# A convolution whose last two channel blocks change PSUM pools, with a statistics step moved between their taps and weight splits held further back

## The chip, the cores and the metric

One core of a Trainium2 chip runs the whole program in one launch. The metric is device time in microseconds (us), the median of several runs. Stretches of the trace are given in us from the start of the profiled span.

## What is computed

Four layers, one after the other, on 256 tokens of width 1024, each followed by a gated feed-forward layer. Everything is float32 in and out; matrix products are done at near-float32 accuracy by splitting each operand into a high and a low part. The change lies in the last mixer, the "conformer" convolution:

```
def conformer_conv(h, w_pw1, b_pw1, w_dw, b_dw, ln_g, ln_b, w_pw2, b_pw2):
    a, gate = jnp.split(h @ w_pw1 + b_pw1, 2, axis=-1)
    u = a * jax.nn.sigmoid(gate)
    dw = lax.conv_general_dilated(u, w_dw[:, None, :], window_strides=(1,),
        padding=((CONV_WIDTH_2 - 1, 0),), ..., feature_group_count=D_MODEL) + b_dw
    mu, var = mean and variance of dw over the channels
    z = jax.nn.silu((dw - mu) * lax.rsqrt(var + EPS) * ln_g + ln_b)
    return z @ w_pw2 + b_pw2
```

The convolution has 31 taps for each of 1024 channels, which lie as 8 blocks (k = 0 to 7) of 128 channels on the partitions and 256 tokens along the free axis.

## The kernel before, in words

The stage (`conformer`) works through a list of steps, `ORDER`: `p` steps project two channel blocks into banks of the pool `acc` (four banks), gate them on ACT (L1193) and DVE (L1195) into a tile `u` and split `u` into `uh` and `ul` (L170 on ACT, L171 on DVE). `c` steps convolve two blocks. Of the 31 taps of a block some (`PE_TAPS`) are done on PE: for each tap a diagonal matrix with the tap's weight, in high and low parts, is the stationary operand, and three matmuls of 128x256 (L335 to L337, high x high, high x low, low x high) sum into one bank of the pool `pw`, two banks. The diagonals are made by ACT (L1140, one 128x128 activation for each half) for blocks 0 to 6, and for block 7 by GpSimd (L1135, one `affine_select` for up to eight taps). They stand in a rotating pool of four tiles. Taps beyond the sixteenth use odd offsets and copies of `uh`, `ul` moved by one (L1222, L1223). The other taps run on DVE, one instruction a tap (L1243 for the first, L1245 for the rest), into `d`; at the end the PE bank is added to `d` (L1248), which sets the bank free.

`s` steps (`stat`) transpose two finished blocks of `d` on PE (L1254) into a bank of the pool `ptr` and take `bn_stats` on DVE (L1257). When all four are done, DVE aggregates (L1276) and adds EPS (`eps`, L1277), GpSimd takes the power -0.5 (L1278), DVE forms the negative mean (`mean`, L1279), and PE spreads both over the partitions into a bank `br` (L1282). Then, for pieces of one, one, two, two and two blocks, DVE multiplies and adds (L1290, L1291; the adds are `adds[0]` to `adds[4]`), ACT applies Silu (L1293) and casts the high part `zTh` (L170), and DVE forms the low part `zTl` (L171). Matmuls of 10 and 7 that compute nothing (L218) run on PE while it waits here.

The output projection (`outproj`) multiplies by `conv_w_pw2` in four chunks of two channel blocks; each chunk is one 1 MB transfer into `raw` (L144, queued on SP, three buffers), and is split in four pieces of 128x512 into `hi` (L164, ACT) and `lo` (L166, DVE), three buffers each. Chunks 0 and 1 go through all banks first; chunks 2 and 3 are the tail, bank by bank, and each finished bank is added to `x` (L411). `self.hold` says behind which DVE instruction the low part of each piece may be issued, for chunks 0, 1 and 2.

Each engine's queue runs in order; the order is fixed when the program is built, from the order of the code, the dependencies, and a lead (`high_priority(offset=...)`): the normalization steps have a lead of 800 (`FIRST`), the splits of chunk 0 of 120, of the other chunks of 1.

Of the kernel before, what the change touches and what calls it, by code (L numbers as in the profile page):

```python
# [17 lines left out]
P = 128  # L18
D = 1024
S = 256  # L20
# [11 lines left out]
TUNE = [(150, 4), (1, 4), (400, 4), (1, 4), (1, 4), (1, 4), (400, 4), (1, 4)]  # L32
XBC = (4, 5, 0, 1, 2, 3)
FIRST = 800
ORDER = "p0 c01 p1 c23 s0 p2 c45 s1 p3 c67 s2 s3"
MORDER = "s0 p0 s1 v0 p1 n1 v1 s2 s3 v2 v3"
PE_TAPS = [13] * 6 + [16, 20]


def f32(ap):  # L40
    return ap.bitcast(F32)


def T(t):
    return slice(t * P, (t + 1) * P)
# [12 lines left out]
class Net:  # L58
# [1084 lines left out]
    def conformer(self, after):  # L1143
# [3 lines left out]
        with self.stage("conf") as sp, self.stage("confp") as pp:  # L1147
            s1 = lambda shape, name, dt=F32, **kw: sp.tile(list(shape), dt, name=name, **kw)
# [55 lines left out]
            def conv(ks):  # L1204

                bs, rest = {}, {}
                if ks[0] == 0:
                    with self.tc.issue_after(self.joint[0]), self.tc.issue_after(self.joint[1]):
                        for i in range(2):
                            n = 16 - i  # L1210
                            self.split(self.whl_dw[:, i, :n, 0], self.whl_dw[:, i, :n, 1], self.wdw[:, i::2])
                for k in ks:
                    u, uh, ul = us[k]
                    n_odd = max(0, PE_TAPS[k] - 16)
                    taps = [list(range(0, 2 * min(PE_TAPS[k], 16), 2)), list(range(1, 2 * n_odd, 2))]
                    rest[k] = [n for n in range(TAPS) if n not in taps[0] + taps[1]]
                    moved = [(uh, ul)]
                    if n_odd:

                        uh1 = sp.tile([P, H + S], F32R, tag="uh1", name="uh1", bufs=1)  # L1220
                        ul1 = sp.tile([P, H + S], F32R, tag="ul1", name="ul1", bufs=1)
                        nc.scalar.copy(uh1[:, :H + S - 1], f32(uh[:, 1:]))  # L1222
                        nc.scalar.copy(ul1[:, :H + S - 1], f32(ul[:, 1:]))  # L1223
                        moved.append((uh1, ul1))
                    b = bs[k] = self.bank("pw", (P, S))
                    left = PE_TAPS[k]
                    for odd in range(2):
                        for t0 in range(0, len(taps[odd]), 8):
                            ts = taps[odd][t0:t0 + 8]
                            with self.tc.issue_after(self.joint[0]):  # L1230
                                dg = self.diags(pp, ts, k)
                            for n, tap in enumerate(ts):
                                c = slice(tap - odd, tap - odd + S)
                                self.mm3W(b, dg[:, 2 * n], dg[:, 2 * n + 1], moved[odd][0][:, c], moved[odd][1][:, c], left == PE_TAPS[k], left == 1)
                                left -= 1
                for n in range(TAPS):
                    for k in ks:
                        if n >= len(rest[k]):
                            continue
                        u, tap, dk = us[k][0], rest[k][n], d[:, k, :]  # L1240
                        w = self.wdw[:, tap, k:k + 1]
                        if n == 0:
                            nc.vector.tensor_scalar(dk, u[:, tap:tap + S], w, self.bdw[:, k:k + 1], op0=ALU.mult, op1=ALU.add)  # L1243
                        else:
                            nc.vector.scalar_tensor_tensor(dk, u[:, tap:tap + S], w, dk, op0=ALU.mult, op1=ALU.add)  # L1245
                with self.tc.high_priority(offset=FIRST if 7 in ks else 0):
                    for k in ks:
                        nc.vector.tensor_add(d[:, k, :], d[:, k, :], bs[k])  # L1248

            def stat(i):  # L1250
                bt = self.bank("ptr", (P, 2, 2, P))
                for j in range(2):
                    for t in range(2):
                        ins = nc.tensor.transpose(bt[:, t, j, :], d[:, 2 * i + j, T(t)], self.ident).ins  # L1254
                with self.tc.high_priority(offset=FIRST if i == 3 else 0):
                  for t in range(2):
                    nc.vector.bn_stats(stats[:, t, i, :], bt[:, t].rearrange("p j l -> p (j l)"))  # L1257
                return ins

            for step in ORDER.split():  # L1260
                if step[0] == "p":
                    proj(int(step[1]))
                elif step[0] == "c":
                    conv([int(x) for x in step[1:]])
                else:
                    turned = stat(int(step[1]))
# [3 lines left out]
            with self.tc.high_priority(offset=FIRST):  # L1270
                with self.tc.issue_after(turned):
                    self.warm(10, "ptr")
                s2 = lambda name, n=1: sp.tile([P, 2, n], F32, tag=name, name=name, bufs=1)
# [3 lines left out]
                eps = nc.vector.tensor_scalar(rm, mv[:, :, 1:2], EPS, None, op0=ALU.add).ins  # L1277
                nc.gpsimd.tensor_tensor(r, rm, self.nhalf[:, :2].rearrange("p (t o) -> p t o", o=1), op=ALU.pow)  # L1278
                mean = nc.vector.scalar_tensor_tensor(rm, mv[:, :, 0:1], -1.0, r, op0=ALU.mult, op1=ALU.mult).ins  # L1279
# [5 lines left out]
            k, adds = 0, []  # L1285
# [11 lines left out]
            for t in range(2):  # L1297
                nc.vector.tensor_add(self.x[t], self.x[t], bp)

            self.hold = [((), (eps, eps, mean, mean)), ((), (adds[1], adds[2], adds[3], adds[3])), ((), (adds[4],) * 4)]  # L1300
            self.outproj(a["conv_w_pw2_2"][0], lambda k, t: (zTh[:, k, T(t)], zTl[:, k, T(t)]), list(range(8)), after, ahead=1, ahead0=120)

    def late_params(self):
# [111 lines left out]
```

## Time and profile before

| | us |
|---|---|
| median of three runs | 1290.64 |
| the three runs | 1293.62, 1290.4, 1290.64 |
| the profiled execution, its own time | 1293.15 |
| its span in the profile | 1291.4 |
| PE busy in the span | 1271.0 |
| DVE busy | 916.0 |
| ACT busy | 768.5 |

The median is what a version is judged by; the profiled execution is one more run, in which 1.75 us lie outside the span. The shares by engine are over all four layers; the conformer takes the stretch from about 978 to 1098 us of the span.

### The profile page before, as it was taken

How to read it: one execution, taken by the hardware profiler on the slowest of the kernel's cores; microseconds unless marked ns; L12 is line 12 of the kernel's file. 1: busy time of each engine (PE TensorE's matmuls, PEld its weight loads, DVE VectorE, ACT ScalarE, POOL GpSimd, SP SyncE). 2: the span in 40 equal slices, each digit the busy share in tenths (PEclk: the TensorE clock that was granted, in tenths of full speed). 3: DMA queues.
4: the chain of work that ended last, by engine and by line, in shares of the span. 5: the costliest groups of instructions: out<-in, count | busy, mean ns of one | idle time of the engine just before them, and what ended most of it. 6: DMA issues, size and time to landing. Idle time of an engine off the chain costs nothing.

```text
span 1291.4 us, 19316 instructions
## 1 busy us (share of the span) xinstructions
PE 1271.0 (98%) x7188; PEld 1094.1 (85%) x7188; DVE 916.0 (71%) x1882; ACT 768.5 (60%) x1758; POOL 55.0 (4%) x106
## 2 busy tenths in 40 slices
PE   9999999999999999999999999999999999999997
PEld 8888878888888867888888888888889998888886
DVE  6966665767764987866746787777557998777643
ACT  6773554666653876666634445666447995666642
POOL 3000000400000000000000000000000010000000
PEclk9999999999999999999999999999999999999999
DMA  8436344766563433766554545656673304655560
GB/s 256 152 113 209 130 173 153 230 196 196 194 235 101 168 98 100 228 196 192 182 202 158 199 145 190 186 184 191 217 238 118 112 2 147 208 183 182 181 222 35
DMA packets 150543, 219.62 MB, mean 170 GB/s; under 512 B 6634, under 2 KB 119426, under 8 KB 150450
## 3 DMA queue, kind: packets, MB, share of 16 engines
q1 hardware_dynamic: 148528, 213.43, 50.9%
q0 software_dynamic: 1920, 4.96, 1.4%
q8 instruction: 56, 0.92, 0.3%
q14 instruction: 37, 0.30, 0.1%
q10 hardware_dynamic: 2, 0.00, 0.0%
HBM read 217.33 MB, written 1.05 MB: 169 GB/s over the span
## 4 chain that ended last, share of the span: by engine, by line
PE 90%; DVE 6%; ACT 3%; issue 1%; POOL 0%; POOLq 0%; DVEq 0%; ACTq 0%
PE acc L342 18%; PE acc L343 9%; PE acc L330 9%; PE acc L385 9%; PE acc L389 9%; PE acc L386 9%; PE pw L342 5%; PE acc L331 5%; PE pw L343 2%; PE acc L337 2%; PE acc L336 2%; PE acc L335 2%; PE ptr L258 2%; DVE lo L166 1%; PE pw L337 1%; PE pw L335 1%
## 5 line engine op out<-in xcount | busy, mean ns | idle before, releaser
L166 DVE TENSOR_TENSOR lo<-raw,hi 128x512 fp32r<-128x512 f32 (+2 forms) x800 | 514.2, 683 | 168.1 <-ACT hi L164 166.7
L164 ACT CAST hi<-raw 128x512 fp32r<-128x512 f32 (+2 forms) x800 | 448.6, 617 | 228.4 <-PE acc L389 84.9
L342 PE MATMUL acc<-xT,hi 128*128 128x512 f32 x1024 | 359.6, 396 | 0.0
L343 PE MATMUL acc<-xT,lo 128*128 128x256 f32 x1024 | 287.7, 281 | 0.0
L342 PEld LDWEIGHTS acc<-xT,hi 128*128 128x128 f32 x1024 | 192.1, 188 | 45.3
L343 PEld LDWEIGHTS acc<-xT,lo 128*128 128x128 f32 x1024 | 193.5, 189 | 0.2
L386 PE MATMUL acc<-lo,hTh 128*128 128x512 f32 x352 | 137.2, 390 | 0.0
L385 PE MATMUL acc<-hi,hTh 128*128 128x512 f32 x352 | 137.0, 389 | 0.0
L389 PE MATMUL acc<-hi,hTl 128*128 128x512 f32 x352 | 113.5, 389 | 0.0
L331 PE MATMUL acc<-hi,xT 128*128 128x512 f32 (+2 forms) x288 | 108.8, 378 | 0.2 <-DVE xT L171 0.2
L330 PE MATMUL acc<-hi,xT 128*128 128x512 f32 (+2 forms) x288 | 108.2, 376 | 0.0
L330 PE MATMUL acc<-lo,xT 128*128 128x512 f32 (+2 forms) x288 | 108.1, 375 | 0.0
L342 PE MATMUL pw<-xT,hi 128*128 128x512 f32 x256 | 89.8, 395 | 0.0
L459 DVE TENSOR_TENSOR s<-s,acc 128x256 f32<-128x256 f32 x128 | 53.3, 417 | 50.9 <-ACT s L458 50.8
L335 PE MATMUL acc<-xT,hi 128*128 128x256 f32 x288 | 81.8, 284 | 0.0
L337 PE MATMUL acc<-xT,lo 128*128 128x256 f32 x288 | 81.7, 284 | 0.1
L336 PE MATMUL acc<-xT,hi 128*128 128x256 f32 x288 | 81.7, 284 | 0.0
L385 PEld LDWEIGHTS acc<-hi,hTh 128*128 128x128 f32 x352 | 66.1, 188 | 13.9
L389 PEld LDWEIGHTS acc<-hi,hTl 128*128 128x128 f32 x352 | 66.1, 188 | 13.6
L386 PEld LDWEIGHTS acc<-lo,hTh 128*128 128x128 f32 x352 | 66.1, 188 | 13.5
L458 ACT COPY s<-acc 128x256 f32<-128x256 f32 x128 | 47.3, 369 | 45.1 <-PE acc L343 45.1
L343 PE MATMUL pw<-xT,lo 128*128 128x256 f32 x256 | 71.8, 280 | 0.0
(432 smaller groups left out, 2004.3 us busy)
## 6 DMA issues: line engine op xcount, KB each, us to landing
raw<-w_in_even SPq DMA_DIRECT2D x22, 1024.0 KB, 5.2
raw<-w_down SPq DMA_DIRECT2D x22, 1024.0 KB, 5.0
raw<-ffn_w_down SPq DMA_DIRECT2D x22, 1024.0 KB, 5.1
raw<-w_gate SPq DMA_DIRECT2D x20, 1024.0 KB, 5.4
raw<-w_up SPq DMA_DIRECT2D x20, 1024.0 KB, 5.6
raw<-ffn_w_gate SPq DMA_DIRECT2D x20, 1024.0 KB, 5.4
raw<-ffn_w_up SPq DMA_DIRECT2D x20, 1024.0 KB, 5.4
raw<-conv_w_pw SPq DMA_DIRECT2D x12, 1024.0 KB, 5.4
```

The costliest lines, as they stand in the source:

```text
L164: nc.scalar.copy(fl(hi)[:, c], fl(raw)[:, c])
L166: nc.vector.tensor_sub(fl(lo)[:, c], fl(raw)[:, c], f32(fl(hi)[:, c]))
L330: return [mm(out, lh, wh, start=first, stop=False).ins, mm(out, lh, wl, start=False, stop=False).ins, mm(out, ll, wh, start=False, stop=la ...
L331: mm(out, ll, wh, start=False, stop=last).ins]
L335: mm(out, wh, xh, start=first, stop=False)
L336: mm(out, wh, xl, start=False, stop=False)
L337: return mm(out, wl, xh, start=False, stop=last).ins
L342: mm(out.rearrange("p a s -> p (a s)"), wh, self.xx[:, k].rearrange("p a s -> p (a s)"), start=first, stop=False)
L343: mm(out[:, 0, :], wl, self.xx[:, k, 0, :], start=False, stop=last)
L385: done.append(nc.tensor.matmul(b, lh, hi[:, j, cs], start=st, stop=False).ins)
L386: done.append(nc.tensor.matmul(b, lh, lo[:, j, cs], start=False, stop=False).ins)
L389: done.append(nc.tensor.matmul(banks[t][h], ll, hi[:, j, cs], start=False, stop=sp).ins)
```

## The change

Four edits. The PE sums of blocks 6 and 7 go to the pool `acc` instead of `pw`. The statistics of blocks 4 and 5 (`s2`) are no longer a step after `c67`; they are traced between the PE taps of block 6 and those of block 7, and their `bn_stats` get the lead of 800 too. Block 7 has 21 PE taps instead of 20, so one tap fewer on DVE. The low parts of chunk 0 of the next weights are held behind `eps`, `mean`, `adds[1]`, `adds[1]` instead of `eps`, `eps`, `mean`, `mean`, and the first of chunk 1 behind `adds[2]` instead of `adds[1]`.

```
-ORDER = "p0 c01 p1 c23 s0 p2 c45 s1 p3 c67 s2 s3"
+ORDER = "p0 c01 p1 c23 s0 p2 c45 s1 p3 c67 s3"
-PE_TAPS = [13] * 6 + [16, 20]
+PE_TAPS = [13] * 6 + [16, 21]
...
-                    b = bs[k] = self.bank("pw", (P, S))
+                    b = bs[k] = self.bank("pw" if k < 6 else "acc", (P, S))
...
+                    if k == 6:
+                        stat(2)
...
-                with self.tc.high_priority(offset=FIRST if i == 3 else 0):
+                with self.tc.high_priority(offset=FIRST if i >= 2 else 0):
...
-            self.hold = [((), (eps, eps, mean, mean)), ((), (adds[1], adds[2], adds[3], adds[3])), ((), (adds[4],) * 4)]
+            self.hold = [((), (eps, mean, adds[1], adds[1])), ((), (adds[2], adds[2], adds[3], adds[3])), ((), (adds[4],) * 4)]
```

## Rows read from the trace of the kernel before

**Rows 1.** The page: busy time by engine, then the chain's shares by engine.
```profile
PE 1271.0 (98%) x7188; PEld 1094.1 (85%) x7188; DVE 916.0 (71%) x1882; ACT 768.5 (60%) x1758; POOL 55.0 (4%) x106
...
PE 90%; DVE 6%; ACT 3%; issue 1%; POOL 0%; POOLq 0%; DVEq 0%; ACTq 0%
```
**Rows 2.** Waits, 1052 to 1099: who waited for whom; us in total, times, longest.
```profile
ACT uh L170 <- DVE u L1195: 2.5, 1, 2.5
...
PE pw L335 <- DVE d L1248: 1.6, 1, 1.6
```
**Rows 3.** PE's timeline, 1053 to 1089: start, length, engine, line, operation, [idle before].
```profile
1053.63 0.36 PE L335 MATMUL pw<-uh,diag 128*128 128x256 f32 x1 [1.57 <-DVE d L1248]
...
1058.56 0.51 PE L337 MATMUL pw<-uh,diag 128*128 128x256 f32 x2 [0.44 <-ACT diag L1140]
...
1067.18 0.28 PE L335 MATMUL pw<-uh,diag 128*128 128x256 f32 x1
...
1067.54 1.11 PE L1254 MATMUL ptr<-ident,d 128*128 128x128 f32 x8
...
1071.90 0.61 PE L1282 MATMUL pw<-ident,rm 128*128 128x128 f32 x4
...
1075.21 0.51 PE L385 MATMUL acc<-hi,zTh 128*128 128x512 f32 x1 [1.14 <-ACT zTh L170]
...
1088.62 0.39 PE L386 MATMUL acc<-lo,zTh 128*128 128x512 f32 x1
```
**Rows 4.** The chain that ended last, 1050 to 1060: start, length, what.
```profile
1053.41 0.41 DVE d L1248
...
1055.36 0.48 DVE d L1245
1055.84 0.41 DVE u L1195
...
1056.27 0.43 ACT uh L170
...
1056.72 1.28 ACT L1201
...
1058.22 0.30 ACT diag L1140
```
**Rows 5.** ACT's timeline, 1052 to 1069: diagonals of block 6, casts of weights.
```profile
1052.47 1.26 ACT L1140 ACTIVATE diag<-ident,whl_dw 128x128 fp32r<-128x128 f32 x4
...
1058.13 3.90 ACT L1140 ACTIVATE diag<-ident,whl_dw 128x128 fp32r<-128x128 f32 x13
...
1064.67 4.26 ACT L164 CAST hi<-raw 128x512 fp32r<-128x512 f32 x8
```
**Rows 6.** DVE's timeline, 1035 to 1081.
```profile
1035.39 8.79 DVE L1245 SCALAR_TENSOR_TENSOR d<-u,wdw,d 128x256 f32<-128x256 f32 x22
...
1056.87 0.45 DVE L171 TENSOR_TENSOR ul<-u,uh 128x286 fp32r<-128x286 f32 x1
1057.24 9.37 DVE L1245 SCALAR_TENSOR_TENSOR d<-u,wdw,d 128x256 f32<-128x256 f32 x21
1066.71 0.42 DVE L1248 TENSOR_TENSOR d<-d,pw 128x256 f32<-128x256 f32 x1
1067.74 0.42 DVE L1248 TENSOR_TENSOR d<-d,pw 128x256 f32<-128x256 f32 x1 [0.61 <-PE pw L337]
1068.18 1.43 DVE L1257 BATCH_NORM_STATS2 stats<-ptr 128x6 f32<-128x256 f32 x4
...
1071.41 1.89 DVE L166 TENSOR_TENSOR lo<-raw,hi 128x512 fp32r<-128x512 f32 x3
1073.22 0.42 DVE L1290 TENSOR_TENSOR d<-d,pw 128x256 f32<-128x256 f32 x1
...
1080.48 1.89 DVE L166 TENSOR_TENSOR lo<-raw,hi 128x512 fp32r<-128x512 f32 x3
```
**Rows 7.** GpSimd's timeline: the first and the third of three selects.
```profile
1044.39 2.01 POOL L1135 TENSOR_SCALAR_AFFINE_SELECT diag<-whl_dw 128x2048 fp32r<-128x2048 f32 x1 [65.37 <-PE pw L337]
...
1056.82 1.45 POOL L1135 TENSOR_SCALAR_AFFINE_SELECT diag<-whl_dw 128x1024 fp32r<-128x1024 f32 x1 [6.32 <-PE pw L337]
```
**Rows 8.** DVE's groups from 1044.3 to 1046.6: busy us, mean ns.
```profile
L1245 DVE SCALAR_TENSOR_TENSOR d<-u,wdw,d 128x256 f32<-128x256 f32 x1 | 1.8, 1781 | 0.0
```
**Rows 9.** SP's queue: the last transfer of these weights; transfers by kind, us to landing.
```profile
1073.33 0.37 SPq L144 DMA_DIRECT2D raw<-conv_w_pw  x1
...
raw<-conv_w_pw SPq DMA_DIRECT2D x1, 1024.0 KB, 5.0
```

## The prediction

> **What bounds the kernel.** I read the page first: PE is busy 98% of the span and holds 90% of the chain that ended last; DVE holds 6% of it and ACT 3% [rows 1]. So a gain can only come where PE stands still, and only as far as PE gets back to work earlier. All that the change touches lies between 1044 and 1099 us, and there I read the waits [rows 2], PE's and DVE's timelines [rows 3, 6] and the chain itself [rows 4]. The reader is to see two places. At 1052 to 1053.63 PE stands for 1.57 us until DVE has added a finished sum out of a `pw` bank [rows 2, 3]. And from 1068.65, where the last transposes end, to 1075.21 PE has only the transposes' successors: statistics, the spread of mean and deviation, matmuls that compute nothing, and the wait for the first `zTh` [rows 3]. That is 6.6 us in which DVE, GpSimd and ACT set the pace. From 1075.21 on PE is full.
>
> **The bank of blocks 6 and 7.** With `acc` PE need not wait for the adds; the four `acc` banks are free by then, since the projection's sums leave them through L1193 and L1195. PE could start block 6 at 1052.0, 1.6 us earlier. Yet the chain does not run through that wait. It runs through DVE's add at 1053.41, on to `u` of block 7 at 1055.84, ACT's `uh` at 1056.27, a table load of 1.28 us and the diagonal at 1058.22 that PE waits for at 1058.56 [rows 3, 4]; DVE is the late one, and ACT stood 2.5 us for `u` [rows 2]. What is late next, once the bank is free: block 6 has 32 diagonals, 13 of them made after 1058.13, so 19 by 1053.73 [rows 5], that is 9.5 taps. A tap is three matmuls, 0.36 us (1067.18 to 1067.54 in [rows 3]). PE would have used them by 1052.0 + 9.5 x 0.36 = 1055.4 and then stand until block 7's `ul` at 1057.3 [rows 6] or the next diagonal. I take 0 for the bank. The other end: DVE must still finish. Its add of block 6 ends at 1066.71 + 0.42 = 1067.13 [rows 6]; it gets two `bn_stats` more before that (half of 1.43, +0.72), loses a tap (8.79 / 22 = 0.40, [rows 6]) and is held by a wider select (below, +0.14), which makes 1067.59. The last add began at 1067.74, after 0.61 us of idle time. So even a PE that is never late brings that add forward by no more than 0.15 us. The bank's value lies between 0 and 0.15 us.
>
> **The 21st tap.** PE gets 0.36 us more, on the chain, since DVE waits for PE at 1067.74; DVE's 0.40 us less is worth nothing there, as it was idle 0.61. GpSimd's third select grows from 1024 to 1280 columns. The 2048-column one took 2.01 us and this one 1.45 [rows 7], so 0.56 x 256 / 1024 = +0.14 us.
>
> **The select moves.** It waits for a diagonal tile that block 6's first eight taps set free. Those would end at 1052.0 + 24 x 0.12 + 0.3 = 1055.2 instead of 1056.8, so it runs from 1055.2 to 1056.8 with 1.45 + 0.14 us, ahead of `u` and `ul` of block 7 and no longer behind them. The first select ran from 1044.39 to 1046.40, and the DVE tap beside it took 1.78 us [rows 7, 8] where the normal pitch is 0.40. The tap in front of `u` (at 1055.36, [rows 4]) would then end at 1056.8 and `u` with it at 1057.2 instead of 1056.25: 0.95 us, or nothing, if the tap starts just ahead of the select; then the tap and the first-tap instruction between `u` and `ul` are held instead. With `ul` behind them the bounds are 0 and 1.4 us. I take 0.6, in between, because start times here agree to within 0.2 us and either order is open. DVE's own end does not move, for it loses this time to a select in both versions. The Trainium skill ("SBUF — State Buffer", Who interferes with whom) has a rule that speaks against this change: a DVE instruction with two SBUF inputs and a GpSimd instruction that reads SBUF exclude each other for the whole instruction, one with a single SBUF input is not held. By that rule the tap is held to the end and `u`, which reads PSUM and one SBUF operand, only by queueing behind it; the row of 1.78 us agrees. By it alone the term would be 0.95 to 1.4, which is the second rival.
>
> **The statistics step.** Four transposes (half of 1.11 us in [rows 3], 0.5) move from the end to PE's idle time after 1055.4, hidden by the wait for block 7's `ul`; if PE gets to them only later they cost up to 0.5 on the chain. `d` of blocks 4 and 5 is ready by 1053.82 [rows 4]. At the end two `bn_stats` remain. Today four run back to back from 1068.18 to 1069.61, the first two over the last two transposes, which end at 1068.65 [rows 3, 6]. Then they would run from 1068.70 to 1069.42: 0.2 us gained.
>
> **End of the convolution, summed:** last add +0.36 (tap) + 0.6 (select) + 0 (bank, transposes) - 0.35 (of the stalls of PE up to 1058.56: 108 matmuls at 0.12 make 12.9 us, and it took 13.9; a third of that 1.0 may close) = +0.6 us, between -0.15 and 0.36 + 1.4 + 0.5 = +2.3. Statistics -0.2.
>
> **The low parts held back.** Between `mean` and the first multiply three low parts run, to 1073.3; the multiply starts at 1073.22, though the spread it needs ended at 1071.90 + 0.61 = 1072.51 [rows 3, 6]. With one low part there the multiply can start at 1072.55: 0.67 us gained, bounds 0.6 and 0.7. The two others and the third of chunk 1 have smaller leads than the multiplies, adds and `zTl`, so they go where chunk 1's went, to 1080.48 [rows 6]: two low parts there end 1.2 us later, at 1081.7, less a shift of 0.27 = 1081.4. Chunk 0's `raw` buffer is free only then, and the transfer of chunk 3 waits for it: it was issued at 1073.33, when the last low part of chunk 0 had ended [rows 6, 9]. SP's queue behind it holds the next layer's weights. Issued at 1081.5 it lands 5.0 us later [rows 9], 1086.5; four casts of 0.53 [rows 5] and low parts of 0.63 [rows 6] behind them give chunk 3's third low part at about 1088.8. PE takes it in the first bank of the tail at 1088.62 [rows 3], or 1088.35 after the shift. So PE stands some 0.5 us. It is 0 if the two low parts find an earlier gap on DVE, and much more if they come later (third rival). I take 0.5.
>
> **Sum and forecast.** +0.6 - 0.2 - 0.67 + 0.5 = +0.2 us: on the profiled execution's own 1293.15 (span 1291.4 and 1.75 around it) 1293.4. That run lies 2.5 us above the median, beside one of the three; two lie at 1290.4 and 1290.6. Carried to the median: 1290.9 us. The forecast's own range is -1.0 (-0.15 - 0.2 - 0.67) to +1.9 (2.3 - 0.2 - 0.67 + 0.5): 1289.6 to 1292.5. A measurement of this kernel can tell about 0.3%, 3.9 us, from no change; all of this is less.
>
> **Rivals.** First, the bank wait counts: PE uses the time, the order on PE fits, chunk 3 is in time. For it speaks that 1.57 us is PE's longest wait here [rows 2]; against it the chain and DVE's end at 1067.59. It gives -1.0 us, 1289.6. Second, the select holds DVE for all of its length in front of `u`, and the transposes fall on the chain: +1.9 us, 1292.5; for it the 1.78 us row. Third, on the other side, late weights: should the two low parts of chunk 0 be put behind those of chunks 1 and 2 too, eight of 0.61 us = 4.9 us later, chunk 3 lands at 1091.4 and PE stands 0.5 + 4.9 = 5.4 us in the tail: 1290.64 - 0.3 + 5.4 = 1295.7. It decides from a release of chunk 0's `raw` at about 1085 on. Against it speaks their lead, 120 against 1. Fourth, the new order of instructions reaches further than these edits, into the next layer, and shortens PE's 6.6 us at 1068 to 1075 by more than half: -4 us, 1286.6; nothing in the rows shows how, since DVE, GpSimd and ACT do the same steps one after the other.
>
> **Chances.** Forecast 0.60, first rival 0.20, second 0.10, third 0.06, fourth 0.04. The first three lie within 0.3%: same 0.90, slower 0.06, faster 0.04. The range leaves out the last two and takes in the run at 1293.6 that the unchanged kernel shows: 1289.0 to 1293.6.
>
> **What would show it.** In the changed trace: no wait of PE for L1248 at 1052, but a new one between 1055 and 1058.5, for `uh`, `ul` or a diagonal; the third select near 1055, beside a DVE tap of over 1 us; the last L1248 0 to 2 us later than 1067.74; one low part between `mean` and the first L1290; the transfer of chunk 3 near 1081 instead of 1073, and a short wait of PE for `lo` or `hi` near 1088. The prediction is wrong if the last L1248 comes well before 1067.6, if chunk 3 is issued before 1076, or if the time leaves 1287 to 1294.5 us.

## The result

The changed kernel took 1301.5 us (median of 1301.92, 1301.5 and 1300.64) against 1290.64. The quotient of these medians is 1.0084; the ratio on record, which goes with the 95% interval of 1.0037 to 1.009 and is used from here on, is 1.0064. Run again later beside 22 runs of the kernel before, it gave 1.0058 [1.0041 to 1.0076]. The forecast of 1290.9 us and the range of 1289.0 to 1293.6 were wrong; the sign was that of the third rival, at another place.

In the profile PE holds 89% of the chain instead of 90% [rows 1]. Lines behind the new step stand two further on: L1248 of before is L1250, L1245 is L1247, L1257 is L1259. The waits of the changed kernel, 1052 to 1099 us (who waited for whom, total, times, longest), against [rows 2]:

```profile
DVE d L1250 <- PE acc L337: 4.3, 1, 4.3
ACT uh L170 <- DVE u L1195: 3.5, 1, 3.5
...
PE acc L386 <- DVE lo L166: 2.1, 1, 2.1
...
PE acc L335 <- ACT uh L170: 1.8, 1, 1.8
...
PE acc L337 <- ACT diag L1140: 1.4, 1, 1.4
```

PE's wait for the bank, 1.57 us, is gone. Three others stand in its place, of 1.8, 1.4 (0.44 before) and 2.1 us, and DVE waits 4.3 us for PE where it waited 0.61. GpSimd's third select, from its timeline:

```profile
1055.43 1.50 POOL L1135 TENSOR_SCALAR_AFFINE_SELECT diag<-whl_dw 128x1280 fp32r<-128x1280 f32 x1 [4.50 <-PE acc L337]
```

The chain that ended last at the same place (start, length, what), which answers to [rows 4]:

```profile
1055.27 0.50 DVE d L1247
1055.79 1.42 DVE d L1247
1057.21 0.41 DVE u L1195
1057.64 0.43 ACT uh L170
1058.09 1.28 ACT L1201
...
1059.59 0.30 ACT diag L1140
1059.93 0.58 PE acc L337
```

The tap of 1.42 us lies beside the select and ends with it, at 1057; `u` of block 7 queues behind. PE's timeline, against [rows 3]:

```profile
1058.21 0.35 PE L335 MATMUL acc<-uh,diag 128*128 128x256 f32 x1 [1.81 <-ACT uh L170]
...
1059.93 0.58 PE L337 MATMUL acc<-uh,diag 128*128 128x256 f32 x1 [1.36 <-ACT diag L1140]
...
1084.97 0.50 PE L386 MATMUL acc<-lo,zTh 128*128 128x512 f32 x1 [2.08 <-DVE lo L166]
```

Between 1056.40 and 1059.93 PE ran one matmul. What came after that is in the busy time by stretch (stretch, its length, busy us and count of PE, PEld, DVE, ACT, POOL, then the granted clock as a share of 2.4 GHz, DMA share, GB/s):

```profile
1050.00:1056.40 6.40, 6.40 (x54) 6.16 (x53) 6.33 (x14) 4.18 (x14) 1.90 (x2) 1.00 0.00 0
1056.40:1059.90 3.50, 0.36 (x2) 0.19 (x1) 3.50 (x9) 2.23 (x5) 0.54 (x1) 0.81 0.00 0
1059.90:1065.50 5.60, 5.57 (x26) 5.57 (x27) 5.60 (x15) 5.60 (x17) 0.00 (x0) 0.51 0.00 0
1065.50:1072.00 6.50, 6.50 (x57) 6.50 (x55) 2.37 (x6) 4.79 (x10) 0.00 (x0) 1.00 0.01 3
...
1084.00:1086.00 2.00, 1.03 (x4) 0.90 (x5) 2.00 (x4) 1.29 (x3) 0.00 (x0) 0.97 0.00 0
1086.00:1088.00 2.00, 2.00 (x6) 1.51 (x6) 2.00 (x5) 0.00 (x0) 0.00 (x0) 0.50 0.65 143
1088.00:1090.00 2.00, 2.00 (x8) 1.58 (x7) 2.00 (x4) 0.00 (x0) 0.00 (x0) 0.68 1.00 382
```

PE is busy throughout 1059.9 to 1065.5 and does 26 matmuls, half of the pace of 57 in 6.5 us that follows: its clock had been taken down to 1.2 GHz. The same happens after the wait at 1084.97. DVE and SP, against [rows 6, 9]:

```profile
1072.30 0.42 DVE L1250 TENSOR_TENSOR d<-d,acc 128x256 f32<-128x256 f32 x1 [4.25 <-PE acc L337]
...
1076.96 0.42 DVE L1292 TENSOR_TENSOR d<-d,pw 128x256 f32<-128x256 f32 x1 [0.45 <-PE pw L1284]
...
1084.23 1.89 DVE L166 TENSOR_TENSOR lo<-raw,hi 128x512 fp32r<-128x512 f32 x3
...
1085.58 0.37 SPq L144 DMA_DIRECT2D raw<-conv_w_pw  x1
```

One measure serves for all that follows: starts counted from `u` of block 6 (1044.50 before, 1044.93 now), up to the first matmul of the next layer. It leaves out the scatter ahead of that point, where `u` of block 6 began between 1042.1 and 1052.1 us in these profiles without an edit there.

| kernel | `u` of 7 | last add | first multiply | first `zTh` matmul | next layer |
|---|---|---|---|---|---|
| before | 11.26 | 23.24 | 28.72 | 30.71 | 53.96 |
| changed | 12.20 | 27.37 | 32.03 | 34.03 | 60.99 |

So of 7.03 us 4.13 are lost up to the last add, 0.82 won up to the first multiply, 0.01 lost up to `zTh`, and 3.71 lost in the output projection.

### The profile page after: what moved, and what is told of

It reads as the page before. It is cut to its first block, busy times and chain, and to the rows that moved or that the text cites. A ratio compares the mean times of both kernels' runs of the same rounds, so it can differ in the third digit from the quotient of the medians.

```text
span 1298.9 us, 19319 instructions
## 1 busy us (share of the span) xinstructions
PE 1275.8 (98%) x7191; PEld 1099.0 (85%) x7191; DVE 915.7 (70%) x1881; ACT 770.0 (59%) x1758; POOL 53.6 (4%) x106
## 4 chain that ended last, share of the span: by engine, by line
PE 89%; DVE 6%; ACT 3%; issue 1%; POOL 0%; POOLq 0%; DVEq 0%; ACTq 0%
PE acc L342 18%; PE acc L343 9%; PE acc L330 9%; PE acc L386 9%; PE acc L389 9%; PE acc L385 9%; PE acc L331 5%; PE pw L342 5%; PE pw L343 2%; PE acc L337 2%; PE acc L336 2%; PE acc L335 2%; PE ptr L258 1%; DVE lo L166 1%; ACT hi L164 1%
```

## The experiments

The theory: the freed bank lets the third select run ahead of `u` of block 7, the late `u` makes PE stand, and the low parts held back make it stand again; the lower clock adds to both. Its rivals: one of the parts carries all of it, or the lower clock does.

### The hold lists alone, the convolution's part alone, the bank alone

On the kernel before, only the new `self.hold`; on the changed kernel, the old `self.hold`; on the kernel before, only the bank:

```
-                    b = bs[k] = self.bank("pw", (P, S))
+                    b = bs[k] = self.bank("pw" if k < 6 else "acc", (P, S))
```

> The kernel before with the new hold lists alone. Theory A (two losses, each with a stall of PE and then a lower clock): the first multiply starts about 0.67 us earlier against the last add, then PE waits some 2 us for a low part of chunk 0, the granted clock falls to the lower level for about 3.5 us, and the next layer begins 2.5 to 3.5 us later: about 1293.5 us. Rival B (the low parts were late only because the convolution was late): 0 to -0.7 us, 1290.

> The changed kernel with the old hold lists. Theory A: the last add of a PE sum comes 4 us later than before, PE at the lower clock for some 7 us in between, no wait for low parts behind it: +3.9 us, about 1294.5. Rival B2 (the low parts are the main loss, the convolution little): within 1 us of before.

> The kernel before with blocks 6 and 7 in the other pool, nothing else. Theory A (the early start turns a 1.6 us wait into a longer one behind the select and u, and the clock falls): PE waits 3 us or more between 1055 and 1060, the clock is at the lower level after it, the last add is 3 to 4 us later, about 1294 us. Rival C (the moved statistics step or the 21st tap does it): under 1 us from before, clock full.

| kernel | ratio, 95% | `u` of 7 | last add | first multiply | first `zTh` matmul | next layer |
|---|---|---|---|---|---|---|
| hold lists alone | 1.0035 [1.0022, 1.0048] | 11.28 | 23.23 | 28.03 | 30.03 | 55.67 |
| convolution alone | 1.0023 [1.0011, 1.0036] | 12.20 | 25.00 | 30.32 | 32.31 | 56.23 |
| bank alone | 1.0019 [0.9998, 1.004] | 11.98 | 25.15 | 30.62 | 32.61 | 55.64 |

With the hold lists alone the multiply comes 0.69 us earlier, as forecast, and PE then stands 2.06 us for a low part; PE's timeline:

```profile
1081.00 0.51 PE L386 MATMUL acc<-lo,zTh 128*128 128x512 f32 x1 [2.06 <-DVE lo L166]
```

Net +1.71 us at the next layer, at a granted clock of 1.00 all through the projection. The convolution alone gives +2.27, with the same two waits as in the changed kernel, but in this profile the clock stayed; PE's timeline, then two stretches:

```profile
1055.59 0.35 PE L335 MATMUL acc<-uh,diag 128*128 128x256 f32 x1 [1.82 <-ACT uh L170]
1057.31 0.38 PE L337 MATMUL acc<-uh,diag 128*128 128x256 f32 x1 [1.36 <-ACT diag L1140]
...
1095.57 1.29 PE L258 MATMUL ptr<-ident,xn 128*128 128x128 f32 x8 [0.51 <-DVE xn L298]
```
```profile
1058.50:1060.00 1.50, 1.50 (x15) 1.50 (x14) 1.50 (x5) 1.50 (x6) 0.00 (x0) 1.00 0.00 0
1060.00:1062.00 2.00, 2.00 (x19) 2.00 (x19) 2.00 (x6) 2.00 (x6) 0.00 (x0) 1.00 0.00 0
```

The last add is 2.37 us earlier than in the changed kernel: that is the price of the clock there. The third row, a wait for `xn` of the next layer's normalization, makes 0.51 of the +2.27; the changed kernel has none. In the run of the bank alone the third select starts at +10.50, as in the changed kernel, and `u` is 0.72 us late, so the freed bank is enough for that, without the moved statistics and the 21st tap. The clock was down there for some 3.5 us:

```profile
1057.00:1058.50 1.50, 1.06 (x5) 0.84 (x6) 1.50 (x5) 1.49 (x5) 0.00 (x0) 0.68 0.00 0
1058.50:1060.00 1.50, 1.50 (x8) 1.50 (x8) 1.50 (x5) 1.50 (x6) 0.00 (x0) 0.50 0.00 0
1060.00:1062.00 2.00, 2.00 (x16) 2.00 (x15) 2.00 (x7) 2.00 (x7) 0.00 (x0) 0.76 0.00 0
```

1.5 x 0.32 + 1.5 x 0.50 + 2 x 0.24 = 1.7 us lost, which leaves a last add at about 23.4 without it: the freed bank buys nothing at the end of the convolution, as forecast. That one part carries all falls: both cost, and 0.35% and 0.23% of some 1292 us make 7.5 together. That the clock is all of it falls as well: 1.71 + 2.27 = 4.0 us come at full clock (3.5 without the wait for `xn`).

### The changed kernel without the bank

```
-                    b = bs[k] = self.bank("pw" if k < 6 else "acc", (P, S))
+                    b = bs[k] = self.bank("pw", (P, S))
```

> The changed kernel with the old banks for blocks 6 and 7; the moved statistics step and the new hold lists stay. Theory: the convolution's loss is gone: TensorE waits for the bank again (about 1.6 us), u of block 7 at +11.3, the last add at +23.0 to +23.6; the loss at the low parts stays (about 2.1 us of TensorE's wait in front of the third low part's matmul), next layer at about +55.5 as in the run of the hold lists alone, so some 4 us over the kernel before. Rival: the moved statistics step itself holds DVE's tap: then u is at +12 and the last add at +25 also without the freed bank.

1.0032 [1.0014, 1.005]; `u` of 7 at 11.26, last add at 24.04, next layer at 57.05. PE's timeline:

```profile
1056.39 0.36 PE L335 MATMUL pw<-uh,diag 128*128 128x256 f32 x1 [1.56 <-DVE d L1250]
...
1059.91 0.60 PE L1256 MATMUL ptr<-ident,d 128*128 128x128 f32 x4
...
1061.33 0.38 PE L337 MATMUL pw<-uh,diag 128*128 128x256 f32 x1 [0.69 <-ACT diag L1140]
...
1083.95 0.51 PE L386 MATMUL acc<-lo,zTh 128*128 128x512 f32 x1 [2.04 <-DVE lo L166]
```

`u` is on time again, so the select follows the bank and the statistics step doesn't hold DVE. But the last add is 0.80 us late, more than expected. The wait for the diagonal ends at 14.07 as before (14.06); by then PE has done 30 matmuls of the two blocks, and the transposes, where it had done 34. With the 21st tap's three that is 7 x 0.12 = 0.84 us more to do behind it. So the rows give 1.76 us for the convolution's part at full clock as 0.94 (late `u`) and 0.82 (this). With the bank alone PE had done 34 too, so the four fewer come with the moved statistics, whose transposes (0.60 us) stand there now, or with the 21st tap; the two were not run apart.

### What makes u late: the select behind it, or u ahead of the taps

In both the old hold lists and the rest of the changed kernel. First, GpSimd copies one column of block 7's `ul` ahead of the third select (nothing uses the copy), so the select runs behind `ul`:

```
+                            if k == 7 and odd:
+                                seen = sp.tile([P, 1], F32, name="seen")
+                                wait = self.tc.issue_after(nc.gpsimd.tensor_copy(seen, f32(ul[:, 0:1])).ins)
```

> The changed kernel with the old hold lists and the third select placed behind the u that GpSimd copies of block 7 (a one-column copy of its low part ahead of the select; that copy computes nothing that is used). Theory: the select is what holds the tap in front of u, so u of block 7 comes about 11.3 us after u of block 6 (12.20 in the run of the convolution's part alone), TensorE's wait ahead of block 7 shrinks from 1.8 us to about 0.9 and the last add comes at about +24.1 (25.00 there) where the clock stays full. Rival: u is late because the freed bank moves DVE's own work in front of it, whatever GpSimd does; then u stays at +12.2 and the last add at +25.0 or later.

Second, the taps of blocks 6 and 7 on DVE are issued behind `ul` of block 7:

```
+                with self.tc.issue_after(self.u_lo) if 7 in ks else nullcontext():
                     for n in range(TAPS):
```

> The changed kernel with the old hold lists, and all DVE taps of blocks 6 and 7 queued behind u and ul of block 7. Theory A (PE waits because u and ul stand behind three tap instructions on DVE, one of them held by the select): u about 2 us earlier than in the changed kernel, PE waits about 1 us instead of 3.2, from the gate of block 6 to the last add 23.2 to 23.7 us against 25.0 without this order and 23.2 before; next layer within 0.5 us of before, about 1291.5. Rival (ACT's making of diagonals is what PE waits for, wherever u stands): still 2.5 us of waiting and 24.7 us or more to the last add.

Third, the second with 22 taps of block 7 on PE in place of 21:

> The u-first form of the convolution's part (u of block 7 ahead of DVE's taps), with 22 instead of the 20 taps of the last block on TensorE. In the u-first run TensorE waited 0.68 us for DVE's last add, so DVE set the end there. Theory: two taps fewer on DVE bring the last add from +23.2 to about +22.9 and the next layer 0.2 to 0.3 us earlier (+55.5 from +55.75, with the stretch behind it at 190.9 us): a time up to 0.4 us under the kernel before, which this measurement hardly tells from no change. Rival: TensorE's two more taps (4 passes of 0.12 us or more, with their two diagonals on ScalarE) bind in DVE's place: last add +23.2 or later.

| kernel | ratio, 95% | `u` of 7 | last add | next layer |
|---|---|---|---|---|
| select behind | 1.0031 [1.002, 1.0042] | 11.26 | 25.55 | 57.34 |
| `u` first | 1.0002 [0.9989, 1.0015] | 9.92 | 23.49 | 55.75 |
| `u` first, 22 taps | 1.0015 [1.0001, 1.0028] | 9.93 | 23.44 | 54.85 |

With the select behind, `u` is on time and PE waits 0.87 us for `uh` instead of 1.8: the select is what held it. The wait for the diagonal stays, and the clock fell after these two as well; PE's timeline, then the stretches:

```profile
1054.48 0.36 PE L335 MATMUL acc<-uh,diag 128*128 128x256 f32 x1 [0.87 <-ACT uh L170]
1056.19 0.38 PE L337 MATMUL acc<-uh,diag 128*128 128x256 f32 x1 [1.36 <-ACT diag L1140]
```
```profile
1057.00:1058.50 1.50, 1.50 (x11) 1.50 (x10) 1.50 (x5) 1.50 (x7) 0.00 (x0) 0.59 0.00 0
1058.50:1060.00 1.50, 1.50 (x9) 1.50 (x9) 1.50 (x5) 1.50 (x5) 0.00 (x0) 0.50 0.00 0
1060.00:1062.00 2.00, 2.00 (x16) 2.00 (x16) 2.00 (x6) 2.00 (x6) 0.00 (x0) 0.83 0.00 0
```

1.5 x 0.41 + 1.5 x 0.50 + 2 x 0.17 = 1.7 us; 25.55 less that is 23.9, near the 24.1 expected at full clock. The times don't show this gain: 1.0031 here, 1.0023 for the convolution alone. With `u` first the select meets `ul` instead, and DVE becomes the late one; its rows, with both adds of blocks 6 and 7 in the second:

```profile
1055.82 1.25 DVE L171 TENSOR_TENSOR ul<-u,uh 128x286 fp32r<-128x286 f32 x1 [0.50 <-ACT uh L170]
...
1068.10 0.75 DVE L1252 TENSOR_TENSOR d<-d,acc 128x256 f32<-128x256 f32 x2
```

`ul` takes 1.25 us where it takes 0.45 [rows 6]. PE's clock stays at 1.00. The add of block 6 starts at 23.16 and the last one, of block 7, at 23.49, 0.25 us later than before; the first multiply, with two `bn_stats` fewer ahead of it, is 0.09 us later (28.81). This is the best form of the convolution's part, and it is no faster than the kernel before. The expectation for the 22nd tap started from +23.2, which is the add of block 6. With it PE's wait for these adds falls from 0.68 to 0.26 us, but the wider select (1536 columns) holds `ul` for 1.48 us, and the last add comes at 23.44, 0.05 us earlier: DVE still sets the end, and the gain of the theory (0.3) isn't there. The next layer of these versions starts up to 1.5 us later than the add suggests, for PE waits for `xn` of the next layer's normalization (1.54 us with `u` first, 0.69 with 22 taps, none before); why that order moved was not tried.

### Matmuls that compute nothing in the wait, to keep the clock

On the changed kernel, 28 and then 14 of the L218 kind between the taps of blocks 6 and 7:

```
                     if k == 6:
-                        stat(2)
+                        with self.tc.issue_after(stat(2)), self.tc.high_priority(offset=FIRST):
+                            self.warm(14)
```

> The changed kernel with 28 matmuls that compute nothing behind the moved transposes, so that PE is busy while it would wait for u and the diagonals. Theory A (the clock is most of the convolution's loss): clock full from 1058 to 1066, last add near 1069 instead of 1072.3, 3 us less than the changed kernel, about 1298.3. Rival D (the wait alone is the loss, the clock small): last add within 0.7 us of the changed kernel's.

> The changed kernel with 14 matmuls that compute nothing behind the moved transposes; the 28 of the run before showed as 56 passes and 6.4 us, twice the wait that they were to cover, so half of them, 3.2 us, should cover it. Theory A (a wait, and in some executions a lower clock after it): clock full, from the gate of block 6 to the last add about 25.0 us, as in the changed convolution at full clock, where the changed kernel's profile has 27.4; the wait for a low part behind it stays. About 2 us under the changed kernel if its timed runs have the lower clock each time, nothing if they seldom have it. Rival (the filler itself is in the way): over 26 us to the last add.

The 28 took 6.4 us, twice the wait, and so don't tell what the wait alone costs: 1.0064 [1.0035, 1.0094], last add at 27.53. The 14 took 3.3 us; PE's timeline, then the stretches:

```profile
1056.25 3.29 PE L218 MATMUL pw<-ones 128*128 128x128 f32 x28
1059.94 0.38 PE L337 MATMUL acc<-uh,diag 128*128 128x256 f32 x1 [0.41 <-ACT diag L1140]
...
1061.41 0.39 PE L335 MATMUL acc<-uh,diag 128*128 128x256 f32 x1
...
1061.99 0.38 PE L335 MATMUL acc<-uh,diag 128*128 128x256 f32 x1
```
```profile
1056.00:1060.00 4.00, 3.59 (x33) 3.40 (x31) 4.00 (x9) 2.32 (x5) 0.95 (x1) 1.00 0.00 0
1060.00:1066.00 6.00, 6.00 (x39) 5.36 (x40) 6.00 (x16) 6.00 (x18) 0.00 (x0) 1.00 0.01 3
```

The clock stays at 1.00 through the taps. One such profile would not show that the fillers do it, since the convolution alone kept its clock too; but all ten timed runs with fillers have a mean granted clock of 0.997 or 0.998, and seven of the nine of the changed kernel 0.994 or 0.995. So the low clock comes of PE's standing still, though not each time. The last add is at 26.44, 0.9 earlier than in the changed kernel, but over the rival's 26: the filler is in the way. PE now does the rest of block 6 in one piece, a tap in 0.58 us (1061.41 to 1061.99) instead of 0.36, the pace at which ACT makes two diagonals (12 in 3.61 us); some six taps of that make the 1.4 us by which it lies behind the convolution alone. The time, 1.0045 [1.0031, 1.0058], can't be told from the changed kernel's. After the low part's wait, which has no filler, the clock fell to 0.50 again in this profile.

### A lead for the low parts

On the kernel before with the new hold lists, and then on the changed kernel with `u` first too, the low parts of chunk 0 get a lead above the multiplies':

```
-                with self.tc.issue_after(parts[i]) if parts else nullcontext():
+                with self.tc.issue_after(parts[i]) if parts else nullcontext(), self.tc.high_priority(offset=2 * FIRST if ahead == 120 else 0):
```

> The kernel before with the new hold lists, and the low parts of chunk 0 with a lead greater than that of the multiplies, so that the third and fourth run right behind the second add. Theory A (their place in DVE's queue, behind the multiplies, makes the loss): no wait of PE for a low part, the transfer of chunk 3 issued within 4 us of the first multiply instead of 8.6, the gain of 0.6 us in front of the multiply kept: next layer 0.3 to 0.7 us earlier than before, about 1291. Rival (holding them behind the adds costs by itself, since they delay the later multiplies): PE waits for zTh or zTl instead, 1 us or more, no gain.

> The changed kernel with both repairs, u and ul of block 7 first and the low parts of chunk 0 with the greater lead. Theory A: all four edits kept and no loss, next layer 0.5 to 1.2 us earlier than before by the last add's place (up to 0.3), the statistics (0.2) and the low parts (0.6); about 1291, faster than the changed kernel by 8 us and from before by less than can be told. Rival (another loss is left in the edits): over 1294.

1.0024 [1.0009, 1.004], next layer at 54.48; and 1.0006 [0.9994, 1.0019], next layer at 54.87. PE's wait for the low part falls from 2.06 to 0.50 us, and chunk 3 is issued at 30.9 us instead of 36.7. But the multiplies behind the low parts come later, and the next layer is still 0.5 to 0.9 us behind the kernel before: holding low parts back gains 0.7 us ahead of `zTh` and loses more behind it, in either order. The expected 0.3 to 1.2 us of gain didn't come. What the second of the two does show is that with both repairs all four edits take the time of the kernel before, so no further loss that this measurement can tell is hidden in them.

### The changed kernel once more

> The changed kernel once more, for a narrower ratio and a second profile. If the lower clock behind TensorE's wait comes in some executions only, this profile either repeats the last add at about +27.4 and the next layer at +61.0 (clock lowered), or shows the last add near +25.0 and the next layer near +58 (clock full). The time by the sum of the two parts run alone (0.35% and 0.23%) is some 7.5 us over the kernel before; by the first three runs 8.3 us.

Last add at 27.56, next layer at 61.21: the lower clock is there again, at both places (0.50 from 1060 to 1064, 0.54 and 0.61 from 1086 to 1090). The granted clock of the timed runs tells much the same, as the mean over the runs of a kernel:

| kernel | runs | mean granted clock |
|---|---|---|
| before | 21, 27, 22 | 0.9978, 0.9979, 0.9981 |
| changed | 6 | 0.9947 |
| changed, 28 and 14 fillers | 5, 5 | 0.9976, 0.9974 |
| convolution alone; bank alone; select behind | 10, 10, 8 | 0.9966, 0.9965, 0.9969 |
| hold lists alone; without the bank | 5, 5 | 0.9972, 0.9974 |
| `u` first; with 22 taps | 11, 10 | 0.9975, 0.9975 |
| lead on the hold lists; both repairs | 11, 11 | 0.9975, 0.9976 |

Against the kernel before of the same chip the changed one lacks 0.0034; times 1295 us that makes 4.4 us at most (where PE stands anyway, a low clock costs nothing). With the 4.0 us of the two parts at full clock it makes up to 8.4, where the two comparisons found 0.64% and 0.58%, 8.3 and 7.5 us. So the lower clock is no accident of the profile. It isn't in every run, though: the first three of the changed kernel had 0.994, 0.994 and 0.998, these six 0.994 to 0.997, and the two runs at 0.997 and 0.998 took 1304.71 and 1301.5 us, no less than the others. The clock's price is thus read from the profiles, where 7.03 us split into 3.0 at full clock (1.76 at the last add, -0.82 up to the multiply, 2.08 for the low part) and 4.0 for the clock (2.37 at the last add, 1.6 in the projection); the timed runs scatter too much to show it run by run.

## Why the prediction was wrong

**The bank: right.** At full clock it is worth nothing at the last add (about 23.4 against 23.24), for the reason given: DVE's end and the chain through `u` set the pace.

**The select moves: place right, term mis-sized.** It was forecast from 1055.2 to 1056.8 and ran from 1055.43 to 1056.93; the tap held by it took 1.42 us, and `u` came at +12.20 instead of +11.26: 0.94, where the working had 0.95 or nothing and "I take 0.6, in between". The order was not open: the select starts at +10.50 and the tap in front of `u` at +10.86, 0.36 us behind it, in the changed kernel and in the convolution alone. The rule cited from the Trainium skill ("SBUF — State Buffer", Who interferes with whom) agrees with the rows: the tap, with two SBUF operands, is held, and with `u` first it is `ul`, with two as well, for 1.25 us. That `u` itself is not held the kernel before shows on block 6, whose `u` lay beside the first select (1044.39 to 1046.40, [rows 7]) and took the same 0.48 us as that of block 7 without one:

```profile
1044.50 0.48 DVE L1195 SCALAR_TENSOR_TENSOR u<-acc,lp,sg 128x256 f32<-128x256 f32 x1 [0.31 <-ACT sg L1193]
...
1055.76 0.48 DVE L1195 SCALAR_TENSOR_TENSOR u<-acc,lp,sg 128x256 f32<-128x256 f32 x1
```

So the working's own 0.95 was right, and the 0.6 a hedge between it and nothing.

**The step that failed first** is the sum of the convolution's end: "0 (bank, transposes) - 0.35 (of the stalls of PE up to 1058.56: ... a third of that 1.0 may close)". PE's stalls did not close, they grew: it stood for 1.81 and 1.36 us where the kernel before has 1.57 and 0.44. The last add came 1.76 us later at full clock (convolution alone) where +0.6 was forecast and +2.3 was the upper bound: 0.36 for the tap as forecast, 0.94 for the select instead of 0.6, and, in place of 0 and -0.35, +0.46, for PE had four matmuls fewer behind it when it stood for the diagonal. The transposes did go into PE's idle time, as forecast, but in the new order four matmuls of block 7 that used to stand ahead of this wait come behind it. DVE's own end came as forecast: its add of block 6 ended at 1067.63 + 0.42 = 1068.05, which is 1067.62 less the later start of 0.43, and 1067.59 was worked out.

**What was missing altogether**, and took the loss past that bound, is the clock. No term and no rival had PE run slower after standing still: 2.37 us at the last add, and about 2 x 0.50 + 2 x 0.32 = 1.6 us in the projection. Without it the profile's loss would be some 3.0 us, 1293.7 on the median before, just outside the range.

**The statistics behind the last add and the low parts ahead of the multiply: right.** -0.2 and -0.67 were forecast, -0.82 came from the last add to the first multiply, 0.69 of it from the hold lists alone.

**The low parts behind: wrong place.** "PE stands some 0.5 us" was put on chunk 3. Its transfer did come late, at 1085.58 instead of 1073.33 (forecast about 1081.4), and PE did not wait for it. It waited 2.08 us for the third low part of chunk 0 itself, which ran at 1084.23 behind the multiplies and `zTl`, where the working had put it (1081.4, and later by the shift), without asking which matmul of PE needs it next. The third rival named late weights of chunk 3, 5.4 us; the loss in the projection was 3.71, by another path.

**Left open.** Why the two waits of 1.8 and 1.4 us took the clock down in both profiles of the changed kernel and not in that of the convolution alone, and the same wait for the low part (2.04 to 2.08) in the changed kernel and not in the profiles of the hold lists alone or without the bank. And the hold lists alone cost 4.5 us in time [2.8 to 6.2] where their profile shows 1.7. Whether the moved statistics or the 21st tap cost the four matmuls ahead of the diagonal was not tried.

## What to carry to other kernels

A wait that is taken away starts everything behind it earlier, also the instruction of a third engine that shares something with the one on the chain: follow each releaser to the next thing that it sets free. A wait on a full PE is not worth its length alone: behind some of the waits here it ran at half pace for 3.5 to 5.6 us. Before work is held back on an engine that is "behind the critical step anyway", look up which matmul of PE's fixed order takes it first.

## What the runs showed of the hardware beyond that

The clock fell after PE had stood 0.87 and 1.36 us with one matmul between (select behind), and did not after 1.57 and 0.44 with 4.5 us of matmuls between (before, [rows 3]). That is no rule: it stayed at 1.00 after 1.82 and 1.36 in the convolution alone, and after a single wait of 2.04 to 2.08 us it fell in the changed kernel and not with the hold lists alone. Each fp32 filler of 128 columns shows as two matmuls: 14 as 28 in 3.29 us.

PE also has two paces at a granted clock of 1.00. In the next layer, the changed kernel's two profiles side by side, first profile, then second:

```profile
1150.00:1170.00 20.00, 20.00 (x115) 17.33 (x115) 14.61 (x29) 13.52 (x31) 0.00 (x0) 1.00 0.53 170
```
```profile
1150.00:1170.00 20.00, 20.00 (x117) 17.64 (x116) 15.18 (x31) 13.18 (x31) 0.00 (x0) 1.00 0.55 169
```

The same program, 2% apart for some 100 us, so that the stretch from the next layer's first matmul to the end is 193.0 us in one and 190.9 in the other. Of the fourteen profiles the second of these and that of `u` first have 190.9, the others 192.9 to 193.4; what decides it was not tried. That, with the scatter of 10 us ahead of the convolution, is why the stretches were compared here and not the totals; single runs of one kernel lie up to 10 us apart.
